# HGRN's f and q projections computed with the tokens stationary and turned through DRAM, in a hybrid decoder trunk

## The chip, the cores and the metric

The kernel runs on one core of a Trainium2 chip. The metric is the time of one execution on the device in microseconds (us); a kernel is timed in several runs and the median is given. The profile is that of one execution. It names the engines PE (TensorE, matmuls; PEld is its loading of the stationary operand), DVE (VectorE), ACT (ScalarE), POOL (GpSimd) and SP (SyncE, which here issues the transfers of the weights and of the output).

## The reference, cut to what matters

One layer on x of 256 tokens by 2048 channels. All projections come from one matrix; three mixers A, B and C each make a branch of 1024 channels, which goes through its block of `w_out` and is added to x under a sigmoid gate.

```python
h = rmsnorm(x, norm_w)
proj = h @ w_in
a_q, a_f, a_i, a_z, b_x, b_z, c_z, c_xbc, c_dt, gate_logits = split(proj)
# A (HGRN2): 8 heads of 128 channels, chunks of 64 tokens, scanned with a state per head
log_f = logaddexp(log(lb), log1p(-lb) + log_sigmoid(a_f)); k = -expm1(log_f)
b = cumsum(log_f)                                 # within the chunk
decay = exp(where(causal, b[t] - b[s], -inf))
scores = einsum('tk,sk,tsk->ts', a_q, k, decay)
o_a = scores @ a_i + (a_q * exp(b)) @ state
o_a = rmsnorm(o_a, hgrn_norm_w) * silu(a_z)
...                                               # B: convolution and a gated scan; C: SSD
branches = stack([o_a, o_b, o_c])
x = x + sum_n sigmoid(gate_logits[n]) * (branches[n] @ w_out[n])
return rmsnorm(x, final_norm_w)
```

## The kernel before, in words

**Precision.** Every large product is made of fp32r matmuls with both sides split into a high and a low part, three products in all (high by high, high by low, low by high). The input times `norm_w` is there as `hT`, 16 slices of 128 channels by 2 parts by 256 tokens. The weights come as tiles `raw` of 128 x 2048 values (1 MB, issued by SP, three buffers). `split(h)` (L394) takes half a tile: ACT casts it to `whi` (L408) and DVE subtracts to get `wlo` (L410). Four buffers each (`WB`) let the splitting run ahead of PE.

**Two forms of block.** `tok_block` (L504) has the tokens stationary: for each of 16 slices and each half of the tokens, three matmuls (L516 to L518) with 128x128 of `hT` stationary and 512 columns of weights moving; 96 matmuls for 512 columns of the projection, and the result lies as tokens by channels. `chan_block` (L454) has the weights stationary and moves `hT`: for each slice and each of two groups of 128 channels one matmul of 512 columns (both parts of `hT` against `whi`, L465) and one of 256 (L466); 64 matmuls for 256 columns of the projection, and the result lies as channels by tokens. PSUM holds two such blocks (`pp`), so a block must have been emptied by the end of the block after it.

**Emptying.** A channel block of f or q is emptied by `copied` and `joined`: ACT copies one half out of PSUM, DVE adds the other and multiplies by `rstd`. Token blocks whose result must lie by channels are emptied by `turned` (x of B and C) or `silu2` (the z gates): ACT scales into a buffer `gt` (two of them), DVE transposes 32x32 blocks into a second `gt`, and POOL's queue writes it to DRAM; `pads_in` and `gates_in` then read it back by POOL's queue as channels by tokens. `gates` keeps tanh of a merge gate in both `gt` buffers until `merged` has used them.

**Order of the work.** `plan()` (L32) lists the blocks; PE runs them in that order without a pause of its own. All other work is written as generator streams. A model clock (`Clock`, `Streams`) advances PE by a constant of the code (0.64 us for three matmuls) and the other engines by formulas; after each such step `quantum` emits those pieces of streams that fit by the model. A piece marked "p" (matmuls of a stream) is placed in PE's queue only where the model has its inputs ready. The order is fixed in the program; on the chip an engine waits where the model was wrong. Transfers enter the model as a fixed delay in `ready`.

**Stages.** C and B come first, up to about 401 us of the span; then stage A: per i from 0 to 3 the channel blocks a_f and a_q (two heads each), for i 0 and 2 the block a_z, and one merge of branch B (a gate block of 96 matmuls and a `wout` block of 48). Then come four merges of branch A. `a_unit(i)` (L1059) is the stream of two heads: ACT and DVE make the logarithms from f, a scan makes `b`, seven levels of products with exponentials follow, then small matmuls on PE, and the result is split into `boh` and `bol`. Tokens such as "A1", "A2", "ls" let one unit use a set of buffers at a time. The first `wout` block of branch A waits for all four units (`force`, `left[0]`).

**The end.** `last_block` (L522) computes the last `wout` block in three parts (token half 0; then token half 1 in two column halves); `last_merge` adds each to x, sums squares, takes the power -0.5 on POOL and scales rows, which SP writes out (`scaled`, L1318).

Of the kernel before, what the change touches and what calls it, by code (L numbers as in the profile page):

```python
# [277 lines left out]
def trunk(ctx, tc, xT, xtok, w, wdt, wax, prm, heads, cst, msk, fnw, out):  # L278
# [175 lines left out]
    def chan_block(name):  # L454

        h0 = 2 * FIRST[name]
        st.room()
        ps = pp.tile([P, 2, 512], F32, name="ps")
        for q in range(4):
            hi, lo = part(h0 + q)  # L460
            for kk in range(4):
                k = q * 4 + kk
                for ct in range(2):
                    c0 = kk * 256 + ct * 128
                    pe.matmul(ps[:, ct], lhsT=hi[:, c0:c0 + 128], rhs=flat(hT[:, k]), start=k == 0, stop=False)  # L465
                    pe.matmul(ps[:, ct, S:], lhsT=lo[:, c0:c0 + 128], rhs=hT[:, k, 0], start=False, stop=k == KD - 1)  # L466
                spent(h0 + q, kk == 3)
        return ps

# [190 lines left out]
    def joined(o, ps):  # L660

        act.copy(out=o, in_=ps[:, :, S:])
        st.after()
        dve.tensor_tensor(out=o, in0=o, in1=ps[:, :, 0:S], op=ALU.add)
        dve.tensor_tensor(out=o, in0=o, in1=rstd.broadcast_to([P, 2, S]), op=ALU.mult)
# [576 lines left out]
    def copied(pool, ps, tag, name):  # L1242
        yield from st.get(tag, "a")
        if tag == "q":

            t = pool.tile([P, 16, 48], F32, name=tag, bufs=2)
            o, ps, r = t[:, :, 0:32].rearrange("p (c g) s -> p c g s", c=2), ps.rearrange("p c (i g s) -> p c i g s", i=2, g=8), rstd.rearrange("p o (g s) -> p o g s", g=8)
            for c in range(2):
                act.copy(out=o[:, c], in_=ps[:, c, 1])
            st.after()  # L1250
            for c in range(2):
                dve.tensor_tensor(out=o[:, c], in0=o[:, c], in1=ps[:, c, 0], op=ALU.add)
            dve.tensor_tensor(out=o, in0=o, in1=r.broadcast_to([P, 2, 8, 32]), op=ALU.mult)
        else:
            t = pool.tile([P, 512], F32, name=tag, bufs=2)
            joined(t.rearrange("p (c s) -> p c s", c=2), ps)
        ready[name] = (t, ck.end)

# [40 lines left out]
    def last_merge(ps, j, c0, c1):  # L1299
# [6 lines left out]
        for _ in merge_in(ps, 0, 3, j, c0, c1):  # L1306
            if n == 4:
                scaled(0, 0, 512, dve)
        if c1 == 512:
# [2 lines left out]
            gp.tensor_tensor(out=tot[:, 1:2], in0=tot[:, 0:1], in1=fin["half"], op=ALU.pow)
# [1 line left out]
        if j == 1:
            for c, w, on in ((512, 512, act), (1024, 512, act), (1536, 512, act)) if n == 3 else ((0, 256, dve), (1024, 512, act), (256, 256, dve), (512, 512, dve), (1536, 512, dve)):
                scaled(n - 3, c, w, on)

    def scaled(j, c, w, on):  # L1318
# [6 lines left out]
        nc.sync.dma_start(out=out[j, :, c:c + w], in_=o)  # L1325

    for name, kind, arg in PLAN:
# [11 lines left out]
        elif kind == "C":  # L1339
            if name == "a_f0":  # L1340
# [5 lines left out]
            ps = chan_block(name)  # L1346
            what, i = name[:3], name[-1]
            st.empty(copied(A[2], ps, what[2], name))
            if what == "a_f":
                st.add(a_unit(int(i)))  # L1350
        elif kind == "T":
# [150 lines left out]
```

## Time and profile before

| what | value |
|---|---|
| median of 3 runs (lowest to highest) | 828.19 us (827.52 to 828.86) |
| the profiled execution's own time | 828.65 us |
| its span, and granted clock of PE | 826.7 us, 0.995 |
| busy share: PE, DVE, ACT, POOL | 98%, 74%, 58%, 11% |
| PE's first block begins, last matmul begins | 5.6 us, 816.8 us |

The profiled execution took 1.95 us more than its span, and 0.46 us more than the median. Matmuls are pipelined: a matmul of 512 columns is shown 389 ns long while the next begins 227 ns later, so durations of PE rows overlap, and what a block costs is read from the starts. A row of the timeline gives start, duration, engine, line, operation, output and inputs, and in brackets the idle time before it and what ended it. Most operations of ACT and DVE stand under L154, the line of a helper, and are told apart by their tiles.

### The profile page before, as it was taken

The numbers are of one execution on the slowest core, as the hardware profiler recorded it, in microseconds if no ns is written. First come the engines' busy times: TensorE is split into PE (matmuls) and PEld (weight loads), VectorE is DVE, ScalarE is ACT, GpSimd is POOL, SyncE is SP. The second block draws the span as 40 slices with busy tenths as digits, with TensorE's granted clock in tenths as the row PEclk, the third lists the DMA queues.
The fourth block names the chain that finished last, engine by engine and source line by source line (L and its number), as shares of the span: only waits on it lengthen the run. The fifth ranks groups of instructions, "written<-read, shape, count | busy, mean of one in ns | idle before, by whom it ended". The sixth has DMA issues, their size and how long they took to land.

```text
span 826.7 us, 12101 instructions
## 1 busy us (share of the span) xinstructions
PE 811.6 (98%) x4677; PEld 678.2 (82%) x4677; DVE 610.2 (74%) x968; ACT 479.0 (58%) x653; POOL 91.7 (11%) x175
## 2 busy tenths in 40 slices
PE   8999999999999999999999999999999999999995
PEld 8978788888888888888888888888888888888884
DVE  6577658888778787878586888689778868656463
ACT  6556445565665676666466565747745673744443
POOL 0000514410520052000100200000020000000000
PEclk9999999999999999999999999999999999999998
DMA  9947676864776587655545744553574555565522
GB/s 339 360 158 249 201 254 215 272 223 179 242 248 246 193 259 250 216 183 190 207 153 204 224 168 171 204 205 125 194 243 153 172 204 186 200 211 201 203 102 101
DMA packets 30088, 171.63 MB, mean 208 GB/s; under 512 B 4960, under 2 KB 5504, under 8 KB 11984
## 3 DMA queue, kind: packets, MB, share of 16 engines
q1 hardware_dynamic: 23360, 153.63, 52.8%
q0 software_dynamic: 6528, 17.16, 7.0%
q8 instruction: 36, 0.59, 0.3%
q10 hardware_dynamic: 144, 0.09, 0.1%
q14 instruction: 20, 0.16, 0.1%
HBM read 163.50 MB, written 7.36 MB: 207 GB/s over the span
## 4 chain that ended last, share of the span: by engine, by line
PE 93%; DVE 2%; DMA 2%; ACT 1%; issue 1%; SPq 0%; POOL 0%; POOLq 0%; DVEq 0%; ACTq 0%
PE ps L516 25%; PE ps L518 25%; PE ps L517 25%; PE ps L465 7%; PE ps L466 3%; PE pmt L154 3%; PE ps L478 2%; DMA xc_t<-xT 1%; DMA xd<-gt 1%; PE pmt L981 1%; DVE wlo L410 1%; ACT whi L408 1%; DVE sc L154 0%; ACT l L154 0%; PE ps L536 0%
## 5 line engine op out<-in xcount | busy, mean ns | idle before, releaser
L410 DVE TENSOR_TENSOR wlo<-raw,whi 128x1024 fp32r<-128x1024 f32 x275 | 333.0, 1220 | 164.3 <-ACT whi L408 162.2
L408 ACT CAST whi<-raw 128x1024 fp32r<-128x1024 f32 x275 | 286.9, 1050 | 285.4 <-PE ps L518 201.3
L516 PE MATMUL ps<-whi,hT 128*128 128x512 f32 x768 | 301.2, 392 | 0.0
L517 PE MATMUL ps<-wlo,hT 128*128 128x512 f32 x768 | 299.1, 389 | 0.0
L518 PE MATMUL ps<-whi,hT 128*128 128x512 f32 x768 | 299.1, 389 | 0.0
L516 PEld LDWEIGHTS ps<-whi,hT 128*128 128x128 f32 x768 | 144.2, 188 | 30.6 <-issue 1.1
L518 PEld LDWEIGHTS ps<-whi,hT 128*128 128x128 f32 x768 | 144.2, 188 | 30.1
L517 PEld LDWEIGHTS ps<-wlo,hT 128*128 128x128 f32 x768 | 144.2, 188 | 29.3
L465 PE MATMUL ps<-hT,whi 128*128 128x512 f32 x256 | 90.6, 397 | 0.0
L466 PE MATMUL ps<-hT,wlo 128*128 128x256 f32 x256 | 71.7, 280 | 0.0
L516 PE MATMUL ps<-whi,boh 128*128 128x512 f32 x176 | 69.2, 393 | 0.0
L518 PE MATMUL ps<-whi,bol 128*128 128x512 f32 x176 | 68.6, 390 | 0.0
L517 PE MATMUL ps<-wlo,boh 128*128 128x512 f32 x176 | 68.5, 389 | 0.0
L465 PEld LDWEIGHTS ps<-hT,whi 128*128 128x128 f32 x256 | 48.0, 188 | 11.3
L466 PEld LDWEIGHTS ps<-hT,wlo 128*128 128x128 f32 x256 | 48.3, 189 | 0.2
L719 POOL DMA_DIRECT2D cpad<-xd x64 | 38.7, 672 | 16.7 <-DMA xd<-gt 7.5
L518 PEld LDWEIGHTS ps<-whi,bol 128*128 128x128 f32 x176 | 33.0, 188 | 6.9
L516 PEld LDWEIGHTS ps<-whi,boh 128*128 128x128 f32 x176 | 33.1, 188 | 6.6
L517 PEld LDWEIGHTS ps<-wlo,boh 128*128 128x128 f32 x176 | 33.1, 188 | 6.5
L154 ACT ACTIVATE gt<-ps,rtok 128x512 f32<-128x512 f32 x44 | 29.5, 683 | 8.7 <-PE ps L518 6.9
L127 ACT ACT_TABLE_LOAD x26 | 33.4, 1283 | 1.6 <-PEq L1495 1.2
L686 POOL DMA_DIRECT2D zd<-gt x12 | 6.7, 560 | 241.1 <-DVE gt L154 177.9
(241 smaller groups left out, 691.2 us busy)
## 6 DMA issues: line engine op xcount, KB each, us to landing
raw<-w SPq DMA_DIRECT2D x137, 1024.0 KB, 4.8
zd<-gt POOLq DMA_DIRECT2D x12, 256.0 KB, 2.7
gz<-zd POOLq DMA_DIRECT2D x48, 64.0 KB, 4.9
raw<-w SPq DMA_DIRECT2D x5, 512.0 KB, 9.0
xsq<-xtok SPq DMA_DIRECT2D x2, 1024.0 KB, 10.9
brd<-sums POOLq DMA_DIRECT2D x4, 512.0 KB, 5.8
xd<-gt POOLq DMA_DIRECT2D x8, 256.0 KB, 2.7
cpad<-xd POOLq DMA_DIRECT2D x64, 32.0 KB, 4.3
```

The source lines that it names most:

```text
L127: self.eng.preload_act_table_set(self.set)
L154: return f(*a, **k)
L408: nc.scalar.copy(out=hi, in_=raw[:, sl])
L410: nc.vector.tensor_tensor(out=lo, in0=raw[:, sl], in1=hi.bitcast(F32), op=ALU.subtract)
L465: pe.matmul(ps[:, ct], lhsT=hi[:, c0:c0 + 128], rhs=flat(hT[:, k]), start=k == 0, stop=False)
L466: pe.matmul(ps[:, ct, S:], lhsT=lo[:, c0:c0 + 128], rhs=hT[:, k, 0], start=False, stop=k == KD - 1)
L478: pe.matmul(ps[:, ct], lhsT=(hi, lo)[i][:, c0:c0 + 128], rhs=hT[:, q * 4 + kk, j], start=q == 0 and n == 0, stop=q == 3 and n == last)
L516: pe.matmul(pss[j], lhsT=hi_ap(k, j), rhs=hi[:, sl], start=k == 0, stop=False)
L517: pe.matmul(pss[j], lhsT=hi_ap(k, j), rhs=lo[:, sl], start=False, stop=False)
L518: pe.matmul(pss[j], lhsT=lo_ap(k, j), rhs=hi[:, sl], start=False, stop=k == nk - 1)
L719: gp.dma_start(out=t[32 * q:32 * q + 32, ct, 3:].rearrange("p (j i s) -> p j i s", j=2, i=4), in_=zd[q, 2 * u + ct])
L981: pe.matmul(o, lhsT=wp[:, a, ct, g], rhs=xp[:, b, ct], start=u == 0, stop=u == 2)
```

## The change

- f and q of a pair of heads become one token block `x_a{i}` of 512 columns (256 of f, 256 of q); `chan_block`, `copied` and `joined` go. The number of weight tiles stays.
- The block is emptied by `turned`; a new stream `heads_in` reads it back with 8 transfers for f and 8 for q. Within f the channels of the two heads now lie interleaved in groups of 32 tokens, and `a_unit` undoes this on the way (`head`, `plain`), writing the log of the gate to a new tile `lf` in the buffer of `l1`; "ls" is given back earlier, "A1" later.
- `turned` scales in place in PSUM and transposes from PSUM, with one `gt` buffer where there were two; `silu2` likewise, and its added wait of 2.5 us of the model goes.
- The plan of stage A: the merge of branch B comes one block later (x_a0, a_z0, x_a1, merge 0, x_a2, a_z1, merge 1, x_a3, merges 2 and 3).
- The end: rows of token half 0 are scaled and written earlier; the square sum of the last part is one DVE operation (`tensor_tensor_reduce`) where it was ACT's and an addition; the last rows are scaled in six pieces, two of them by ACT, which issues their transfers on its own queue.

```diff
     for i in range(4):
-        c(f"a_f{i}", (A_F + i * 256, 256))
-        c(f"a_q{i}", (A_Q + i * 256, 256))
+        t(f"x_a{i}", (A_F + i * 256, 256), (A_Q + i * 256, 256))
         if i % 2 == 0:
             t(f"a_z{i // 2}", A_Z + i * 256)
-        merge(1, i)
+        if i:
+            merge(1, i - 1)
+    merge(1, 3)
...
     def silu2(ps, name):
...
-            dve.scalar_tensor_tensor(out=u, in0=ps[j], scalar=1.0, in1=u, op0=ALU.add, op1=ALU.mult)
-            if j == 1:
-                st.cur.t = max(st.cur.t, ck.end) + 2.5
-                yield "v"
-
-            r = gpool.tile([P, 512], F32, name="gt")
-            dve.transpose(out=r.rearrange("p (q w s) -> p w q s", q=4, w=4), in_=u.rearrange("p (w q s) -> p w q s", q=4, w=4))
-            gp.dma_start(out=zds[name][:, j], in_=r)
+            dve.scalar_tensor_tensor(out=ps[j], in0=ps[j], scalar=1.0, in1=u, op0=ALU.add, op1=ALU.mult)
+
+            dve.transpose(out=u.rearrange("p (q w s) -> p w q s", q=4, w=4), in_=ps[j].rearrange("p (w q s) -> p w q s", q=4, w=4))
+            gp.dma_start(out=zds[name][:, j], in_=u)
...
     def turned(ps, name):
...
-            u = gpool.tile([P, 512], F32, name="gt")
-            act.activation(out=u, in_=ps[j], func=AF.Copy, scale=rtok[:, 0, j:j + 1])
+            act.activation(out=ps[j], in_=ps[j], func=AF.Copy, scale=rtok[:, 0, j:j + 1])
             yield "v"
             r = gpool.tile([P, 512], F32, name="gt")
-            dve.transpose(out=r.rearrange("p (q w s) -> p w q s", q=4, w=4), in_=u.rearrange("p (w q s) -> p w q s", q=4, w=4))
+            dve.transpose(out=r.rearrange("p (q w s) -> p w q s", q=4, w=4), in_=ps[j].rearrange("p (w q s) -> p w q s", q=4, w=4))
...
+    def heads_in(name, i):
+
+        yield from flagged(name)
+        zd = zds.pop(name).rearrange("(i c) j (q w s) -> q w c j i s", i=4, q=4, w=4)
+        yield from st.get("f", "")
+        f = A[2].tile([P, 512], F32, name="f", bufs=2)
+        f5 = f.rearrange("p (j i w s) -> p w j i s", j=2, i=4, w=2)
+        for q in range(4):
+            for w in range(2):
+                gp.dma_start(out=f5[32 * q:32 * q + 32, w], in_=zd[q, w])
+        ready[f"a_f{i}"] = (f, st.cur.t + 12.0)
...
+        ready[f"a_q{i}"] = (t, st.cur.t + 18.0)
...
-        for h, sl in hs:
-            dve.scalar_tensor_tensor(out=ls[:, sl], in0=ls[:, sl], scalar=lnlb[:, h:h + 1], in1=f[:, sl], op0=ALU.max, op1=ALU.add)
+        lf = a1.tile([P, 512], F32, tag="l1", name="lf")
+        for ct, (h, sl) in enumerate(hs):
+            dve.scalar_tensor_tensor(out=plain(lf, ct), in0=head(ls, ct), scalar=lnlb[:, h:h + 1], in1=plain(f, ct), op0=ALU.max, op1=ALU.add)
         st.put("f")
-        st.put("A1")
+        st.put("ls")
...
     def last_merge(ps, j, c0, c1):
...
+        if n == 3 and j == 1:
+
+            scaled(0, 512, 512, act, nc.sync)
+            scaled(0, 1024, 512, dve, nc.sync)
...
+            scaled(0, 1536, 512, act, nc.sync)
...
+            dve.tensor_tensor_reduce(out=g, in0=xa, in1=xa, scale=1.0, scalar=tot[:, 0:1], op0=ALU.mult, op1=ALU.add, accum_out=tot[:, 0:1])
...
+        if j == 0:
+            scaled(0, 0, 512, act, nc.sync)
+        elif n == 4:
+            for c, w, on, q in ((512, 512, act, nc.scalar), (1536, 256, act, nc.scalar), (0, 256, dve, nc.sync), (256, 256, dve, nc.sync), (1024, 512, dve, nc.sync), (1792, 256, dve, nc.sync)):
+                scaled(1, c, w, on, q)
```

More of the change, by code (lines that the diff above doesn't have):

```diff
@@ L70 @@
 PLAN = plan()
-NT = {"C": 2, "CC": 4, "T": 4, "O": 2}
+NT = {"CC": 4, "T": 4, "O": 2}
 FIRST = {}
@@ L452, in spent @@
         st.quantum()
[L454 to L468, printed above, removed]
     def first_quarter(ps, q, hi, lo, h):
@@ L658, in until @@
         return t
[L660 to L665, printed above, removed]
     zds = {}
@@ L720, in pads_in @@
             ready[part] = (t, st.cur.t + 10.0 + 8.0 * u)
+    def heads_in(name, i):
[8 more added lines that the diff above has]
+        ready[f"a_f{i}"] = (f, st.cur.t + 12.0)
+        yield from st.get("q", "")
+        t = A[2].tile([P, 16, 48], F32, name="q", bufs=2)
+        for q in range(4):
+            for w in range(2):
+                gp.dma_start(out=t[32 * q:32 * q + 32, 8 * w:8 * w + 8, 0:32].rearrange("p (j i) s -> p j i s", j=2), in_=zd[q, 2 + w])
+        ready[f"a_q{i}"] = (t, st.cur.t + 18.0)
     def gates_in(pool, name):
@@ L1086, in a_unit @@
         yield "v"
-        for h, sl in hs:
-            dve.scalar_tensor_tensor(out=ls[:, sl], in0=ls[:, sl], scalar=lnlb[:, h:h + 1], in1=f[:, sl], op0=ALU.max, op1=ALU.add)
+        lf = a1.tile([P, 512], F32, tag="l1", name="lf")
+        for ct, (h, sl) in enumerate(hs):
+            dve.scalar_tensor_tensor(out=plain(lf, ct), in0=head(ls, ct), scalar=lnlb[:, h:h + 1], in1=plain(f, ct), op0=ALU.max, op1=ALU.add)
         st.put("f")
-        st.put("A1")
+        st.put("ls")
         yield from st.get("A2", "v")
@@ L1095, in a_unit @@
         fo = a1.tile([P, 256], F32, name="fo")
-        dve.tensor_tensor_scan(b, cc("scan"), ls, 0.0, op0=ALU.mult, op1=ALU.add)
-        act.activation(out=fo, in_=halves(ls, 1)[1][:, :, 0], func=AF.Exp)
-        st.put("ls")
+        dve.tensor_tensor_scan(b, cc("scan"), lf, 0.0, op0=ALU.mult, op1=ALU.add)
+        act.activation(out=fo, in_=halves(lf, 1)[1][:, :, 0], func=AF.Exp)
+        st.put("A1")
         dve.tensor_tensor(out=c, in0=lk, in1=b, op=ALU.subtract)
@@ L1240, in trunk @@
     xacc, fin, gts = {}, {}, {}
[L1242 to L1257, printed above, removed]
     def values(ps, i):
@@ L1305, in last_merge, with scaled @@
             dve.tensor_scalar(out=tot[:, 0:1], in0=tot[:, 0:1], scalar1=D * EPS, scalar2=None, op0=ALU.add)
-        for _ in merge_in(ps, 0, 3, j, c0, c1):
-            if n == 4:
-                scaled(0, 0, 512, dve)
+        cl = slice(3 * 512 + c0, 3 * 512 + c1)
+        xa, g = xacc[0][:, j, cl], gts[j][:, c0:c1]
+        dve.scalar_tensor_tensor(out=g, in0=g, scalar=1.0, in1=ps[:, c0:c1], op0=ALU.add, op1=ALU.mult)
+        dve.scalar_tensor_tensor(out=xa, in0=g, scalar=0.5, in1=xa, op0=ALU.mult, op1=ALU.add)
+        if n == 3 and j == 1:
+            scaled(0, 512, 512, act, nc.sync)
+            scaled(0, 1024, 512, dve, nc.sync)
+            t = fin["pool"].tile([P, 512], F32, name="fsq", bufs=2)
+            act.activation(out=t[:, c0:c1], in_=xa, func=AF.Square, accum_out=fin["fs"][:, j, n:n + 1])
+            scaled(0, 1536, 512, act, nc.sync)
+        elif j == 0:
+            t = fin["pool"].tile([P, 512], F32, name="fsq", bufs=2)
+            act.activation(out=t, in_=xa, func=AF.Square, accum_out=fin["fs"][:, j, n:n + 1])
+            dve.tensor_tensor(out=tot[:, 0:1], in0=tot[:, 0:1], in1=fin["fs"][:, j, n:n + 1], op=ALU.add)
+        else:
+            dve.tensor_tensor_reduce(out=g, in0=xa, in1=xa, scale=1.0, scalar=tot[:, 0:1], op0=ALU.mult, op1=ALU.add, accum_out=tot[:, 0:1])
         if c1 == 512:
-            dve.tensor_tensor(out=tot[:, 0:1], in0=tot[:, 0:1], in1=fin["fs"][:, j, n:n + 1], op=ALU.add)
             gp.tensor_tensor(out=tot[:, 1:2], in0=tot[:, 0:1], in1=fin["half"], op=ALU.pow)
         weigh(3, j, c0, c1)
[L1314 to L1318, printed above, removed]
+        if j == 0:
[3 more added lines that the diff above has]
+                scaled(1, c, w, on, q)
+    def scaled(j, c, w, on, queue):
         o, r = xacc[0][:, j, c:c + w], fin["tot"][:, j, 1:2]
@@ L1324, in scaled @@
             act.activation(out=o, in_=o, func=AF.Copy, scale=r)
-        nc.sync.dma_start(out=out[j, :, c:c + w], in_=o)
+        queue.dma_start(out=out[j, :, c:c + w], in_=o)
     for name, kind, arg in PLAN:
@@ L1338, in trunk @@
             branch_out(1)
-        elif kind == "C":
-            if name == "a_f0":
+        elif kind == "T":
+            if name == "x_a0":
                 st.force(lambda: left[1] == 0 and not st.list)
@@ L1345, in trunk @@
                 branch_out(0)
[L1346 to L1351, printed above, removed]
             ps = tok_block(name, h_hi, h_lo, KD)
@@ L1354, in trunk @@
                 st.empty(values(ps, int(name[-1])))
+            elif name[:3] == "x_a":
+                st.empty(turned(ps, name))
+                st.add(heads_in(name, int(name[3])))
+                st.add(a_unit(int(name[3])))
             elif name[:2] == "x_":
```

21 lines of the change are left out of this document (10 added, 11 removed).

## The prediction

> **What bounds the kernel now.** I read first the page's span, busy times and the chain of work that ended last.
>
> ```profile
> span 826.7 us, 12101 instructions
> PE 811.6 (98%) x4677; PEld 678.2 (82%) x4677; DVE 610.2 (74%) x968; ACT 479.0 (58%) x653; POOL 91.7 (11%) x175
> ...
> PE 93%; DVE 2%; DMA 2%; ACT 1%; issue 1%; SPq 0%; POOL 0%; POOLq 0%; DVEq 0%; ACTq 0%
> ```
>
> PE is busy all the way and makes 93% of the chain. So time is won only where PE streams less, where PE waits, and in the tail after its last matmul. Next the view of waits, of PE alone; its columns are time in all, times, longest.
>
> ```profile
> PE pmt L154 <- DVE ce L154: 1.8, 1, 1.8
> ...
> PE pmt L154 <- DVE sc L154: 1.1, 2, 0.9
> ```
>
> ```profile
> ACT whi L408 <- PE ps L518: 201.3, 143, 3.9
> ```
>
> After its start PE waits three times: 1.8 us once for `ce` (stage C), 1.1 us in two waits for `sc` (units of stage A). The second fence, from the view of all waits, says that the splitting of weights is ahead: ACT waits for PE to give a buffer back, not PE for ACT.
>
> **Part 1: what PE streams for f and q.** The timeline of PE gives the step of each form: first a channel block (stage A), then a token block.
>
> ```profile
> 403.76 0.40 PE L465 MATMUL ps<-hT,whi 128*128 128x512 f32 x1
> ...
> 408.71 0.40 PE L465 MATMUL ps<-hT,whi 128*128 128x512 f32 x1
> ```
>
> ```profile
> 429.82 0.39 PE L518 MATMUL ps<-whi,hT 128*128 128x512 f32 x1
> ...
> 432.54 0.39 PE L518 MATMUL ps<-whi,hT 128*128 128x512 f32 x1
> ```
>
> ```profile
> L465 PE MATMUL ps<-hT,whi 128*128 128x512 f32 x256 | 90.6, 397 | 0.0
> L466 PE MATMUL ps<-hT,wlo 128*128 128x256 f32 x256 | 71.7, 280 | 0.0
> ```
>
> Between the first two rows lie 14 pairs (L465 and L466): 4.95 us / 14 = 0.3536 us a pair. Between the other two lie 12 matmuls: 2.72 / 12 = 0.2267 us each. There are 256 pairs in all (the page's count): 256 x 0.3536 = 90.5 us. They become 4 blocks of 96 matmuls: 384 x 0.2267 = 87.1 us. Removed 90.5, added 87.1: **-3.4 us**, all of it on the path. Both forms move the same columns (64 pairs of 768 columns, or 96 matmuls of 512, are 49,152 for each i); only the number of matmuls falls, from 512 to 384. So the gain is a fixed cost of some 27 ns for each of 128 matmuls, and no fewer columns.
>
> [...]
>
> **Part 2: the wait for `ce`.** Timelines of DVE and of PE around it:
>
> ```profile
> 82.35 1.22 DVE L410 TENSOR_TENSOR wlo<-raw,whi 128x1024 fp32r<-128x1024 f32 x1
> 88.53 0.71 DVE L154 STREAM_TRANSPOSE gt<-gt 128x512 f32<-128x512 f32 x1 [4.96 <-DMA xd<-gt]
> ```
>
> ```profile
> 92.84 0.39 PE L518 MATMUL ps<-whi,hT 128*128 128x512 f32 x1
> 95.06 0.44 PE L154 MATMUL pmt<-ce,xdt 128*64 128x256 f32 x2 [1.84 <-DVE ce L154]
> ```
>
> This is `turned` for x_c0. It takes four `gt` buffers in turn from a pool of two, so the second transpose must wait till the first half has left for DRAM: DVE stands still for 4.96 us, and `xdt`, `ce` and the splits are queued behind it. With the scaling done in PSUM each half takes one buffer, and nothing is in the way. What follows on DVE can come 4.96 us earlier, and PE needs 1.84 of it; 3.1 us are left for what then waits for ACT's next split, whose turn PE sets. **-1.8 us.** What is late next there is PE itself. At the other blocks emptied so the same wait is shorter and no PE wait stands behind it: nothing.
>
> **Part 3: emptying.** From the answers for the tiles f, q and gt (minimum, median, maximum in ns):
>
> ```profile
> L154 ACT COPY f<-ps x4: 573/578/580, 413.6 to 638.2; 128x512 f32<-128x512 f32 x4
> L154 DVE TENSOR_TENSOR f<-f,ps x4: 680/682/689, 414.9 to 639.7; 128x512 f32<-128x512 f32 x4
> L154 DVE TENSOR_TENSOR f<-f,rstd x4: 691/693/694, 415.6 to 640.4; 128x512 f32<-128x512 f32 x4
> ```
>
> ```profile
> L154 ACT COPY q<-ps x8: 354/371/377, 424.9 to 651.9; 128x256 f32<-128x256 f32 x8
> L154 DVE TENSOR_TENSOR q<-q,ps x8: 414/416/422, 426.6 to 652.7; 128x256 f32<-128x256 f32 x8
> L154 DVE TENSOR_TENSOR q<-q,rstd x4: 691/692/693, 427.4 to 653.1; 128x512 f32<-128x512 f32 x4
> ```
>
> ```profile
> L154 ACT ACTIVATE gt<-ps,rtok x44: 669/682/692, 79.6 to 806.4; 128x512 f32<-128x512 f32 x44
> ...
> L154 DVE STREAM_TRANSPOSE gt<-gt x20: 703/706/712, 81.5 to 604.1; 128x512 f32<-128x512 f32 x20
> ```
>
> For each i DVE loses 0.68 + 0.69 + 2 x 0.42 + 0.69 = 2.9 us and gains two transposes, 1.4: over four, -6 us. ACT loses 0.58 + 2 x 0.37 = 1.3 and gains 2 x 0.68: nothing. A transpose that reads PSUM, an ACT result written to PSUM and DVE writing PSUM in `silu2` have no row. The nearest are the DVE additions that read PSUM (682 ns) against the same size from SBUF (693): so 0.68 to 0.71. At twice that, the eight transposes of stage A cost 5.6 us of DVE, about what DVE has gained. The strided halves in `a_unit` keep count and size. All this is on engines with room:
>
> ```profile
> 400.00:720.00 320.00, 318.94 (x2310) 267.42 (x2309) 246.97 (x450) 192.85 (x278) 11.64 (x22) 1.00 0.54 186
> ```
>
> The window of stage A shows PE busy 318.94 of 320 us, DVE 246.97, ACT 192.85. Part 3: 0, hidden beside PE's stream.
>
> **Part 4: the way through DRAM.** Per i the change adds two writes and 16 reads on POOL's queue. The nearest rows are those of x_b1, with the same pieces (32 KB, runs of 32 tokens), from the timelines of DVE and POOL and the list of transfers:
>
> ```profile
> 287.26 0.71 DVE L154 STREAM_TRANSPOSE gt<-gt 128x512 f32<-128x512 f32 x1 [1.77 <-DMA xd<-gt]
> ```
>
> ```profile
> 288.27 0.55 POOL L703 DMA_DIRECT2D xd<-gt  x1 [5.35 <-DVE gt L154]
> ...
> 291.54 4.86 POOL L719 DMA_DIRECT2D cpad<-xd  x8 [2.61 <-DMA xd<-gt]
> ```
>
> ```profile
> cpad<-xd POOLq DMA_DIRECT2D x64, 32.0 KB, 4.3
> ```
>
> The transpose ends at 287.97, the eighth read is issued by 296.40 and lands 4.3 us later, 300.7: f is there 12.7 us after its transpose, q after eight more issues (4.86 us) at about 17.6. The program orders the unit's first step 12 of its own us later, q's use 18; its PE runs at 0.64 us for three matmuls where the chip takes 0.68, so this is 12.8 and 19.1 us of the chip. They fit to a tenth and to 1.5 us. Queued behind the unit's first step on ACT are the splits; buffers for four halves, each used for 12 matmuls (2.72 us), cover three halves less one split (DVE 1.22, ACT counted alike): 8.2 - 2.4 = 5.8 us. Part 2's DVE stall of 4.96 made PE wait for `ce`, not for a split, which agrees. Cost: 0.
>
> [...]
>
> **Part 5: unit 3 and the join.** The first `wout` block of A needs all four units:
>
> ```profile
> 428.89 1.22 DVE L154 TENSOR_TENSOR_SCAN b<-cs,ls 128x512 f32<-128x512 f32 x1
> ...
> 493.93 0.68 DVE L154 TENSOR_TENSOR bol<-osq,boh 128x512 fp32r<-128x512 f32 x1
> ...
> 511.49 1.22 DVE L154 TENSOR_TENSOR_SCAN b<-cs,ls 128x512 f32<-128x512 f32 x1
> ...
> 712.87 0.69 DVE L154 TENSOR_TENSOR bol<-osq,boh 128x512 fp32r<-128x512 f32 x1 [0.69 <-ACT boh L154]
> ```
>
> ```profile
> 740.33 0.39 PE L516 MATMUL ps<-whi,boh 128*128 128x512 f32 x1
> ```
>
> From unit 0's scan to the last unit's end (713.56) are 284.7 us, with 26.8 us to spare before the join. Now unit 0 begins later: its block ends after 96 x 0.2267 = 21.8 us, not 11.3 (32 pairs), and f takes 12.7 us where copy and two DVE passes took 2.7 (413.6 to 416.3, the f rows): some 21 us. The join comes 3.4 us earlier. That would leave 2.4. But the units follow one another through "A2", and between unit 0's end and unit 1's scan lie 16.9 us (494.61 to 511.49), because unit 1's f came late. Now x_a1 ends two blocks, 43.5 us, after x_a0, well within unit 0's 66 us (428.89 to 494.61), so that gap closes and about 19 us are to spare. No price; the strips of DVE between units are filled, which can shift pieces for PE (rivals).
>
> **Part 6: the tail.** Timelines of DVE, ACT and POOL after the last matmul, SP's last two transfers, and the DMA in a window:
>
> ```profile
> 817.55 0.42 DVE L154 SCALAR_TENSOR_TENSOR xacc<-gt,xacc 128x256 f32<-128x256 f32 x1
> ```
>
> ```profile
> 818.07 0.42 ACT L154 ACTIVATE fsq<-xacc 128x256 f32<-128x256 f32 x1 [0.41 <-DVE xacc L154]
> ```
>
> ```profile
> 818.86 0.67 POOL L1312 TENSOR_TENSOR tot<-tot,half 128x1 f32<-128x1 f32 x1 [4.00 <-DVE tot L154]
> ```
>
> ```profile
> 821.34 0.90 SPq L1325 DMA_DIRECT2D out_dram<-xacc  x2
> ```
>
> ```profile
> 822.00:823.00 1.00, 0.00 (x0) 0.00 (x0) 0.00 (x0) 0.00 (x0) 0.00 (x0) 0.50 1.03 370
> ```
>
> From the end of `xacc` (817.97) to POOL are 0.89 us through ACT and a DVE addition. The fused DVE sum has no row; nearest is the 256-element DVE pass, 0.42, so 0.5 with the hand-over; twice that pass would eat the gain. -0.35. Against it, ACT now scales two pieces of half 0 before the third square sum, which may hold DVE back 0.1. SP's last issue ends at 822.24; with four issues on SP and two on ACT it would end some 0.8 earlier. But at 822 the transfer engines are full (370 GB/s), and the last 1 MB needs 2.8 us at that rate whoever issues it; so of this I take 0.15. Together **-0.4 us**, from +0.5 to -1.2.
>
> **Sum.** -3.4 - 1.8 - 0.4 = -5.6 us from the profiled execution's 828.65 (span 826.7), so 823.0. That execution was 0.46 above the median, 828.19: **822.6 us**.
>
> **The rivals.**
> *The two waits for `sc` go too* (1.1 us): they hang on where the program sets PE's pieces, and all of stage A is ordered anew. For: DVE has 6 us less. Time: 821.5.
> *New waits of that kind*: eight such places in stage A, the worst was 0.9. Three or four at 0.5 to 0.9 give 1.5 to 3.5 us: 824.1 to 826.1. For: the units close up, and the order of the z and merge blocks around them is new.
> *Columns alone set the price* of part 1, so that it saves nothing: 826.0. Against: the steps above are regular over 14 pairs and 12 matmuls. [...]
> *Slower: f comes late at ACT.* Place: the first step of each unit, ACT waiting for the eight reads with the splits behind it. Price: what exceeds 5.8 us, four times. To use up the 5.6 us gained it must be 5.8 + 1.4 = 7.2 us late, 20 us after the transpose in place of 12.7; at 9 us late it is four times 3.2, so 835.4. Against: the landings of x_b1, and POOL is idle there (11.64 us of 320).
> *The change does not do what it says*: DVE stalls at 82 us all the same, behind some other buffer: 824.4.
>
> **Chances.** Forecast 0.45 (821.9 to 823.4); `sc` waits gone 0.17; new waits 0.22; columns alone 0.04; DVE stall kept 0.05; f late or the join missed 0.04; the rest, 0.03, is a tail at the outer ends. A measurement of this kernel tells about 0.2% from no change, 1.7 us. Faster by more than that, below 826.5: 0.92. Within: 0.04. Slower: 0.04. The range goes from 820.2 (both `sc` waits gone, tail near -1.2, and a little) to 826.0 (new waits of 3.4 us).
>
> **What would show it.** Right: no L465; the four x_a blocks stepping at 0.227 us; no DVE idle on xd near 83 us and no wait of PE for `ce`; f landing 12 to 13 us after its transpose; POOL's last power about 0.5 us after `xacc`; PE waits of at most 1 to 2 us in stage A. Wrong: PE waiting for whi, wlo or `sc` by more than 4 us between 400 and 720; ACT idle on f for over 6 us; a gap before the first `wout` block of A; transposes from PSUM much over 0.7 us.

## The result and the profile after

The changed kernel takes 832.92 us (median of six runs, 831.88 to 836.83) against 828.42 us for the kernel before (six runs, 827.47 to 828.86): a ratio of 1.0057 [1.0042, 1.0072]. It is 4.5 us slower, where the prediction had it 5.6 us faster. The profiled execution took 831.97 us. The head of its page, then its chain of work:

```profile
span 830.2 us, 11965 instructions
PE 811.4 (98%) x4549; PEld 672.4 (81%) x4549; DVE 605.7 (73%) x957; ACT 486.4 (59%) x652; POOL 134.4 (16%) x247
...
PE 84%; issue 4%; DMA 4%; DVE 3%; ACT 3%; POOL 2%; SPq 0%; POOLq 0%; ACTq 0%; DVEq 0%
```

PE has 128 instructions fewer and is shown busy as long as before. Its share of the chain fell from 93% to 84%: DMA, ACT, DVE and POOL now stand in it. The view of waits of PE, then of ACT (time in all, times, longest):

```profile
PE pmt L152 <- ACT whi L406: 3.9, 2, 2.6
PE pmt L152 <- DVE sc L152: 2.0, 1, 2.0
...
PE ps L499 <- DVE wlo L408: 0.8, 2, 0.5
```

```profile
ACT l L152 <- DMA q<-xd: 10.1, 4, 3.5
```

`ce` is gone from the list. In its place PE waits 6.7 us in stage A, and ACT, which before waited for f once (2.26 us, for DVE's part of the emptying), stands 10.1 us at the first step of the four units (`l` is computed from f; the row names q's transfers, which share POOL's queue).

The window of stage A that the prediction showed, now of the changed kernel:

```profile
400.00:720.00 320.00, 313.26 (x2158) 257.43 (x2157) 238.02 (x435) 197.66 (x275) 54.75 (x94) 0.99 0.56 193
```

PE works 313.26 of 320 us where it was 318.94, at a clock of 0.99 in place of 1.00. DVE has 9 us less to do than before (238.02) and ACT 5 us more (197.66), so neither has become the bound by its work.

**Where the time went**, by the starts of PE's blocks in the two profiled executions:

| stretch | before, us | after, us | difference |
|---|---|---|---|
| to the first token block | 30.89 | 31.22 | +0.33 |
| the next three token blocks (the `ce` wait lies in the third) | 73.37 | 71.43 | -1.94 |
| the rest of C, and B | 297.04 | 297.77 | +0.73 |
| stage A, to the start of its last block | 404.31 | 409.58 | +5.27 |
| last block and end | 21.1 | 20.2 | -0.9 |

The loss is in stage A. Whether the gain of the last row is the change's isn't settled: from the last matmul's start to the end of the span lie 9.9 us before and 9.0 after, but with the new end alone (the run e4_tail, below) 10.0.

Stage A itself. The x_a blocks are what part 1 said. Timeline of PE, first matmul of x_a0 and first of the block behind it:

```profile
400.42 0.39 PE L498 MATMUL ps<-whi,hT 128*128 128x512 f32 x1
...
422.18 0.39 PE L498 MATMUL ps<-whi,hT 128*128 128x512 f32 x1
```

21.76 us for 96 matmuls, 0.2267 each; the two channel blocks took 22.60 (401.30 to 423.90). So 4 x 0.84 = 3.4 us are won, and 8.6 us are lost elsewhere in the stage. The largest piece of the loss is at 491 us. First POOL, with the last transpose of x_a1 on DVE ahead of it (unit 1's f on its way through DRAM):

```profile
470.89 0.71 DVE L152 STREAM_TRANSPOSE gt<-ps 128x512 f32<-128x512 f32 x1
```

```profile
471.89 0.56 POOL L673 DMA_DIRECT2D xd<-gt  x1 [2.15 <-DVE gt L152]
477.00 4.86 POOL L701 DMA_DIRECT2D f<-xd  x8 [4.55 <-issue]
```

POOL stands 4.55 us between the write and the first read. The bracket names no releaser here; in units 0 and 3, where the same gap is 3.26 and 4.98 us, it names the landing of the write (2.61 us at x_b1, in the prediction's row). The eight issues take the 4.86 us that the prediction gave them, and f is there when ACT goes on. ACT's timeline, then DVE's:

```profile
485.83 0.63 ACT L152 ACTIVATE l<-f 128x512 f32<-128x512 f32 x1 [2.50 <-DMA q<-xd]
486.49 1.30 ACT L152 ACTIVATE l<-l 128x512 f32<-128x512 f32 x2
487.69 0.25 ACT L152 COPY sc<-pmt 128x128 f32<-128x128 f32 x1
487.84 1.05 ACT L406 CAST whi<-raw 128x1024 fp32r<-128x1024 f32 x1
```

```profile
487.82 0.69 DVE L152 SCALAR_TENSOR_TENSOR ls<-f,l 128x512 f32<-128x512 f32 x1 [3.24 <-ACT l L152]
...
489.53 0.88 DVE L152 SCALAR_TENSOR_TENSOR lk<-f,ln1lb,l 128x256 f32<-128x256 f32 x2
490.33 0.22 DVE L152 TENSOR_TENSOR dg<-pmt,cs 128x64 f32<-128x64 f32 x1
...
492.81 0.79 DVE L152 COPY sc<-dg 32x64 f32<-32x64 f32 x4
```

ACT has f 14.2 us after the end of its transpose (485.83 less 471.60; units 0, 2 and 3: 14.0, 12.9, 15.5). ACT stands 2.50 us. Behind ACT, DVE stands 3.24 us at unit 1's `ls`. And behind `ls` in DVE's order is not a split but the last work of unit 0: `dg` and `sc`, the scores of its head, whose matmul already stands at the front of PE's queue:

```profile
490.76 0.39 PE L500 MATMUL ps<-whi,bol 128*128 128x512 f32 x1
493.74 1.40 PE L152 MATMUL pmt<-sc,vt 128*128 128x256 f32 x4 [2.59 <-ACT whi L406]
494.79 0.78 PE L498 MATMUL ps<-whi,boh 128*128 128x512 f32 x1
495.36 0.63 PE L499 MATMUL ps<-wlo,boh 128*128 128x512 f32 x1
495.79 0.63 PE L500 MATMUL ps<-whi,bol 128*128 128x512 f32 x1
```

The bracket names ACT's `whi`, but the last cast before it had ended at 488.9; what ends at 493.60, 0.14 us before PE goes on, is DVE's `sc`. So this is a wait for `sc`. And it costs more than its 2.59 us: the next matmuls of 512 columns step by up to 0.57 us, not 0.23. The windows around it (the third number from the right is the clock granted to PE):

```profile
493.50:494.00 0.50, 0.26 (x1) 0.29 (x2) 0.47 (x2) 0.48 (x2) 0.00 (x0) 0.98 0.00 0
494.00:497.00 3.00, 3.00 (x25) 2.06 (x28) 2.77 (x4) 2.73 (x4) 0.00 (x0) 0.50 0.00 0
497.00:497.50 0.50, 0.50 (x48) 0.50 (x42) 0.00 (x0) 0.50 (x2) 0.00 (x0) 0.61 0.00 0
497.50:498.00 0.50, 0.50 (x69) 0.50 (x59) 0.47 (x1) 0.21 (x1) 0.00 (x0) 1.00 0.35 98
```

After the wait the clock is at half (0.50) for 3.4 us, while PE works: another 1.7 us. The kernel before had no such stretch in stage A (1.00). Two more waits of this kind follow for unit 1's head (1.28 and 2.04 us, at 555 and 565 us), without a drop of the clock (1.00), and 0.8 us for `wlo` in unit 3.

The sum of stage A: 404.31 - 3.36 (part 1) + 6.15 (waits, from start to start of the matmuls around them: 7.53 us after, 1.38 before) + 1.70 (half clock) = 408.8; measured 409.58. The remaining 0.8 lies spread over the stretches with small matmuls and was not followed further.

### The profile page after: what moved, and what is told of

It is laid out like the page before. It is cut to its first block, busy times and chain, and to the rows that moved or that the text cites. A ratio compares the mean times of both kernels' runs of the same rounds, so it can differ in the third digit from the quotient of the medians.

```text
span 830.2 us, 11965 instructions
## 1 busy us (share of the span) xinstructions
PE 811.4 (98%) x4549; PEld 672.4 (81%) x4549; DVE 605.7 (73%) x957; ACT 486.4 (59%) x652; POOL 134.4 (16%) x247
## 4 chain that ended last, share of the span: by engine, by line
PE 84%; issue 4%; DMA 4%; DVE 3%; ACT 3%; POOL 2%; SPq 0%; POOLq 0%; ACTq 0%; DVEq 0%
PE ps L498 26%; PE ps L499 26%; PE ps L500 26%; PE pmt L152 3%; PE ps L460 2%; DMA q<-xd 2%; POOL f L701 1%; DMA xc_t<-xT 1%; ACT whi L406 1%; PE pmt L969 1%; DMA xd<-gt 1%; DMA wx<-wax 1%; ACT l L152 1%; POOL gz L718 1%; DVE wlo L408 0%
## 5 line engine op out<-in xcount | busy, mean ns | idle before, releaser
L498 PE MATMUL ps<-whi,hT 128*128 128x512 f32 x896 | 351.8, 393 | 0.0
L499 PE MATMUL ps<-wlo,hT 128*128 128x512 f32 x896 | 348.9, 389 | 0.0
L500 PE MATMUL ps<-whi,hT 128*128 128x512 f32 x896 | 348.8, 389 | 0.0
L498 PEld LDWEIGHTS ps<-whi,hT 128*128 128x128 f32 x896 | 168.2, 188 | 35.5 <-issue 1.1
L500 PEld LDWEIGHTS ps<-whi,hT 128*128 128x128 f32 x896 | 168.2, 188 | 35.2
L499 PEld LDWEIGHTS ps<-wlo,hT 128*128 128x128 f32 x896 | 168.3, 188 | 33.8
L673 POOL DMA_DIRECT2D xd<-gt x16 | 8.9, 555 | 225.6 <-DVE gt L152 220.2
L718 POOL DMA_DIRECT2D gz<-zd x48 | 26.2, 553 | 36.9 <-DVE osq L152 15.9
L152 ACT ACTIVATE gt<-ps,rtok 128x512 f32<-128x512 f32 x36 | 24.0, 684 | 8.3 <-PE ps L500 6.9
L701 POOL DMA_DIRECT2D f<-xd x32 | 19.4, 693 | 15.2 <-DMA xd<-gt 8.2
L707 POOL DMA_DIRECT2D q<-xd x32 | 19.9, 774 | 4.1 <-DMA f<-xd 2.9
L152 DVE STREAM_TRANSPOSE gt<-ps 128x512 f32<-128x512 f32 x28 | 19.9, 712 | 0.4
```

The costliest lines, as they stand in the source:

```text
L152: return f(*a, **k)
L498: pe.matmul(pss[j], lhsT=hi_ap(k, j), rhs=hi[:, sl], start=k == 0, stop=False)
L499: pe.matmul(pss[j], lhsT=hi_ap(k, j), rhs=lo[:, sl], start=False, stop=False)
L500: pe.matmul(pss[j], lhsT=lo_ap(k, j), rhs=hi[:, sl], start=False, stop=k == nk - 1)
L701: gp.dma_start(out=f5[32 * q:32 * q + 32, w], in_=zd[q, w])
L707: gp.dma_start(out=t[32 * q:32 * q + 32, 8 * w:8 * w + 8, 0:32].rearrange("p (j i) s -> p j i s", j=2), in_=zd[q, 2 + w])
```

## The experiments

**Theory A**: f lands after ACT has come to a unit's first step; what stands in order behind that step (the `sc` of the unit before, the splits) comes late, and PE waits. Take away f's lateness alone and stage A loses its waits. **Theory B**: the units now close up and the order of the z and merge blocks is new; PE's small matmuls would wait for DVE in this denser order even if f came in time.

**e1_later** tells the program that f and q come later, and changes nothing else.

```diff
-        ready[f"a_f{i}"] = (f, st.cur.t + 12.0)
+        ready[f"a_f{i}"] = (f, st.cur.t + 16.0)
...
-        ready[f"a_q{i}"] = (t, st.cur.t + 18.0)
+        ready[f"a_q{i}"] = (t, st.cur.t + 22.0)
```

> Edit: only the two delays by which the changed kernel orders the use of f and q after their way through DRAM, 12 and 18 of the program's own us, become 16 and 22. Theory A (ACT stands 2 to 3.5 us in front of the unit's first step because f lands late; the copies to sc of the unit before are queued behind it, and PE's small matmuls wait for those): ACT's four waits on f (10.1 us) shrink to under 2 us in all, PE's waits in stage A fall from 8 us to 1 to 3, time 826 to 829. Rival B (the new order of stage A is too dense for DVE, with or without a late f): the waits of ACT go, PE's waits for sc stay at 6 to 9 us, time 831 to 835.

Measured: 846.25 us, 1.0201 [1.0183, 1.0219]. Neither expectation came true. ACT's waits for f are gone, as they should be, but the delay moves every later piece of the units, and these became longer: from the scan to `bol` 69, 82 and 72 us in three of them, where the changed kernel takes 60, 65 and 64. The last unit ends at 731.7 us, and the join comes too early:

```profile
708.13 0.65 PE L152 MATMUL pmt<-ql,kx 128*32 128x128 f32 x8 [7.29 <-DVE ql L152]
713.71 1.62 PE L152 MATMUL pmt<-sc,vt 128*128 128x256 f32 x4 [3.46 <-DVE sc L152]
720.84 1.62 PE L152 MATMUL pmt<-sc,vt 128*128 128x256 f32 x4 [3.46 <-DVE sc L152]
723.86 0.80 PE L1210 MATMUL pmt<-two,onesr 128*128 128x512 f32 x1 [1.40 <-ACT two L152]
```

15.6 us of waits, and from 704.8 to 728.7 us the clock is at half (0.50 in the window from 705 to 725), which takes 6.1 us more of PE's working time. So this kernel says nothing on A or B; it says that the delay in the program is no knob for one wait: it reorders four units.

**e2_static** leaves all instructions in their order and takes away f's lateness alone: f and q are read from an array that has been in DRAM from the start.

```diff
-        zd = zds.pop(name).rearrange(...)
+        zd = (xtok[:, :, 512 * i:512 * i + 512], zds.pop(name))[0].rearrange(...)
```

> Edit: f and q are read by the same 16 transfers from the input x, which is there from the start, instead of from what the block has written; the writes stay, and the order of every instruction on every engine is that of the changed kernel, so only the wait for the written block goes (the values of f and q are then not those of the projection). Theory A: f lands 3 to 5 us earlier, ACT does not wait for it, PE's waits in stage A fall from 8 us to 1 to 3, time 826 to 829. Rival B (the order itself): time 831 to 834, with the waits for sc still there.

Measured: 826.08 us, 0.9965 [0.9953, 0.9978]. ACT doesn't wait for f, PE's waits in stage A fall to 2.5 us (two for `sc`), the clock stays at 1.00, and stage A takes 403.16 us in place of 409.58. Theory A holds and B falls as the main cause; of B the two `sc` waits remain.

**e3_psum** is the kernel before with the new `turned` and `silu2` alone (and, as in the change, eight DRAM buffers `xd` for four); **e4_tail** the kernel before with the new last block alone.

```diff
-            act.activation(out=u, in_=ps[j], func=AF.Copy, scale=rtok[:, 0, j:j + 1])
+            act.activation(out=ps[j], in_=ps[j], func=AF.Copy, scale=rtok[:, 0, j:j + 1])
...
-            dve.scalar_tensor_tensor(out=u, in0=ps[j], scalar=1.0, in1=u, op0=ALU.add, op1=ALU.mult)
+            dve.scalar_tensor_tensor(out=ps[j], in0=ps[j], scalar=1.0, in1=u, op0=ALU.add, op1=ALU.mult)
```

> Edit: the kernel before with only the new turned and silu2 (scaling and transposing in PSUM, one gt buffer for each half, no added wait of 2.5). By the step of the prediction: PE's wait of 1.84 us for ce near 93 us goes, so 826.4 to 826.8. From the changed kernel's trace: 2.0 us gained there, 0.7 lost again between 320 and 367 us, where wx stands behind gz on POOL's queue: 827.1. If it does nothing: 828.4.

```diff
+            dve.tensor_tensor_reduce(out=g, in0=xa, in1=xa, scale=1.0, scalar=tot[:, 0:1], op0=ALU.mult, op1=ALU.add, accum_out=tot[:, 0:1])
...
+            for c, w, on, q in ((512, 512, act, nc.scalar), (1536, 256, act, nc.scalar), ...):
+                scaled(1, c, w, on, q)
```

> Edit: the kernel before with only the new last block (order of scaling, one DVE sum, six last pieces, two of them issued by ACT). The prediction's step: 0.4 us less, 828.0. From the changed kernel's trace, where last matmul to end of span is 9.03 us and was 9.92: 0.9 less, 827.5.

Measured: e3_psum 827.74 us, 0.9985 [0.9976, 0.9994]; the wait for `ce` is gone. e4_tail 829.28 us, 1.0008 [0.9999, 1.0017]: alone, the new end brings no gain that shows.

**e5_f4 and e6_f16** change in how many transfers f is read, and nothing in the order of PE, ACT and DVE. In e5_f4 both halves of a 64-token run go in one transfer: four of 64 KB. In e6_f16 it is sixteen of 16 KB.

```diff
-        f5 = f.rearrange("p (j i w s) -> p w j i s", j=2, i=4, w=2)
+        f5 = f.rearrange("p (j i m) -> p j i m", j=2, i=4)
         for q in range(4):
-            for w in range(2):
-                gp.dma_start(out=f5[32 * q:32 * q + 32, w], in_=zd[q, w])
+            gp.dma_start(out=f5[32 * q:32 * q + 32], in_=zf[q])
```

> Edit: the changed kernel with f read in 4 transfers of 64 KB (runs of 256 B) in place of 8 of 32 KB; the order on PE, ACT and DVE is unchanged. Theory A (what counts is when f lands, since ACT stands before the unit's first step and PE's small matmuls of the unit before wait for what is queued behind): four issues of 0.6 us less, so f lands some 2.4 us earlier, ACT's four waits on f fall from 10.1 us to 1 to 3, PE's waits in stage A from 8 us to 3 to 4, time 827 to 829. Rival C (the write to DRAM and its landing set the time, the number of reads does not): 832 to 833.

```diff
-            for w in range(2):
-                gp.dma_start(out=f5[32 * q:32 * q + 32, w], in_=zd[q, w])
+            for w in range(2): gp.dma_start(out=f5[32 * q:32 * q + 32, w, 0], in_=zd[q, w, :, 0])
+            for w in range(2): gp.dma_start(out=f5[32 * q:32 * q + 32, w, 1], in_=zd[q, w, :, 1])
```

> Edit: the changed kernel with f read in 16 transfers of 16 KB; the order on PE, ACT and DVE is unchanged. The suspected cost made larger. Theory A: eight more issues of 0.6 us, f lands some 4.9 us later; ACT's four waits rise from 10 to 30 us, and three of the four (units 1 to 3, with small matmuls of the unit before in PE's queue) pass it on to PE: 832.9 + 3 x 4.9, so 843 to 848. Rival C: 832 to 834. By the prediction's cover of 5.8 us for the splits alone the waits of about 7.5 us would cost 4 x 1.7: 839.

Measured: 826.03 us, 0.9963 [0.995, 0.9976], and 843.11 us, 1.017 [1.0153, 1.0188]. The waits of PE, first of e5_f4, then of e6_f16:

```profile
PE pmt L152 <- DVE sc L152: 2.5, 2, 1.6
```

```profile
PE pmt L152 <- ACT whi L406: 11.0, 2, 8.2
PE ps L498 <- ACT whi L406: 2.4, 1, 2.4
...
PE ps L499 <- DVE wlo L408: 0.8, 1, 0.8
```

The first step of the four units on ACT, in e5_f4 (no bracket: no wait) and in e6_f16:

```profile
440.11 0.63 ACT L152 ACTIVATE l<-f 128x512 f32<-128x512 f32 x1
483.69 0.62 ACT L152 ACTIVATE l<-f 128x512 f32<-128x512 f32 x1
544.26 0.62 ACT L152 ACTIVATE l<-f 128x512 f32<-128x512 f32 x1
629.19 0.62 ACT L152 ACTIVATE l<-f 128x512 f32<-128x512 f32 x1
```

```profile
442.89 0.63 ACT L152 ACTIVATE l<-f 128x512 f32<-128x512 f32 x1 [2.88 <-DMA f<-xd]
491.71 0.63 ACT L152 ACTIVATE l<-f 128x512 f32<-128x512 f32 x1 [8.13 <-DMA q<-xd]
556.37 0.63 ACT L152 ACTIVATE l<-f 128x512 f32<-128x512 f32 x1 [3.43 <-DMA f<-xd]
647.74 0.63 ACT L152 ACTIVATE l<-f 128x512 f32<-128x512 f32 x1 [6.35 <-DMA f<-xd]
```

With the changed kernel between them this is a series:

| transfers for f | ACT waits for f | half clock, PE's working time lost | stage A | median |
|---|---|---|---|---|
| 4 | 0 us | 0 us | 403.15 us | 826.03 us |
| 8 (the change) | 10.1 us | 1.7 us | 409.58 us | 832.92 us |
| 16 | 20.8 us | 4.7 us | 420.78 us | 843.11 us |

From 8 to 4 transfers stage A wins 6.4 us: 4.7 of waits (7.53 to 2.82 from start to start) and 1.7 of clock. That is the cause, shown with the change's own order. Both runs went the way of theory A and not of C, but the sizes were off. e5_f4 came out 1 us below its range. e6_f16 lies in its range (843 to 848) in part by luck: ACT's waits came to 20.8 us and not 30, and the half clock, which stood in no sum, made up for it. The series also says what covers a wait and what doesn't. Unit 0's wait (2.26 us in the change, 2.88 in e6_f16) costs PE nothing: no other unit's small matmuls are queued, only splits, and their buffers hold that long. Unit 3's costs little, 1.15 us of 3.46, and 3.56 of 6.35 in e6_f16, through `whi` and `wlo`: the buffers cover 2.3 to 2.8 us. Unit 1's 2.50 us cost 2.75 and then 1.7 of clock: `sc` has no cover at all.

**e7_turned** is the kernel before with the new `turned` alone; **e8_f4_oldsilu** is e5_f4 with the old `silu2`. They are to say which of the two edits costs the 0.7 us in the rest of C and in B. In `silu2`'s new order `wx` stands on POOL's queue behind eight issues of the gates (4.38 us in the changed kernel), and PE waits for `wp`, which is made from it.

```diff
-            act.activation(out=u, in_=ps[j], func=AF.Copy, scale=rtok[:, 0, j:j + 1])
+            act.activation(out=ps[j], in_=ps[j], func=AF.Copy, scale=rtok[:, 0, j:j + 1])
```

> Edit: the kernel before with only the new turned, silu2 as before. If the 0.7 us lost between 320 and 367 us with both edits comes from silu2's new order (wx behind gz on POOL's queue), it is not lost here: PE's wait for ce goes (2.0 us) and nothing is added, 826.6 to 827.0. If it comes from turned, the same 827.7 as with both.

```diff
-            dve.scalar_tensor_tensor(out=ps[j], in0=ps[j], scalar=1.0, in1=u, op0=ALU.add, op1=ALU.mult)
+            dve.scalar_tensor_tensor(out=u, in0=ps[j], scalar=1.0, in1=u, op0=ALU.add, op1=ALU.mult)
+            if j == 1:
+                st.cur.t = max(st.cur.t, ck.end) + 2.5
+                yield "v"
...
+            r = gpool.tile([P, 512], F32, name="gt")
```

> Edit: the changed kernel with f read in 4 transfers and silu2 as before. Theory A: as with 4 transfers alone, less the 0.7 us between 320 and 367 us: 826 to 828.5; the order of stage A shifts a little around the z blocks, which can add or take a wait of 1 to 2 us.

Measured: e7_turned 827.53 us, 0.9978 [0.9969, 0.9987], against 0.9985 for e3_psum: the intervals overlap, so the times don't decide between the two expectations, and the traces don't either. PE's wait for `wp` is 0.2 us with the new `silu2` (the change, e3_psum) and absent with the old one (e7_turned, e8_f4_oldsilu). But the rest of C and B take 297.04 and 297.07 us with both edits out (before, e4_tail), 297.58 and 297.28 with the new `turned` alone (e7_turned, e8_f4_oldsilu), and 297.63 to 298.61 in the nine profiles with both. So a part of the loss is there without the new `silu2` too, profiles with the same code differ by 1 us, and the cause of the 0.7 us stays open. e8_f4_oldsilu 826.57 us, 0.9967 [0.9955, 0.998]: its stage A starts at 400.05 us in place of e5_f4's 400.88 and takes 404.13 us in place of 403.15. ACT waits 3.62 us there for the last unit's f, and PE 3.1 us where it was 2.5; that the one brings the other was not tried.

**e9_f4_early, e10_f4_late and e11_f4_oldplan** start from e5_f4. The first two set the program's delays 1.5 us down and up; the last puts the merges of branch B back directly behind each pair.

```diff
-        ready[f"a_f{i}"] = (f, st.cur.t + 12.0)
+        ready[f"a_f{i}"] = (f, st.cur.t + 10.5)
...
-        ready[f"a_q{i}"] = (t, st.cur.t + 18.0)
+        ready[f"a_q{i}"] = (t, st.cur.t + 16.5)
```

> Edit: f in 4 transfers, and the program orders the use of f and q 1.5 of its own us earlier (10.5 and 16.5). Theory A: f now lands before ACT needs it, with an unknown margin; if that is under 1.6 us, ACT waits again by up to 1.6 us a unit and PE by up to 3 us in all. The 2.5 us that PE still waits for sc depend on where the order puts pieces and can fall or rise by 1 to 2 us. 824.5 to 829.

```diff
-        ready[f"a_f{i}"] = (f, st.cur.t + 12.0)
+        ready[f"a_f{i}"] = (f, st.cur.t + 13.5)
...
-        ready[f"a_q{i}"] = (t, st.cur.t + 18.0)
+        ready[f"a_q{i}"] = (t, st.cur.t + 19.5)
```

> Edit: f in 4 transfers, and the program orders the use of f and q 1.5 of its own us later (13.5 and 19.5). No wait for f. If the units only shift by 1.5 us they make the join (unit 3 ended 27 us before it): 824.5 to 827.5. If what cost 13 us with delays of 16 and 22 (each unit 8 to 17 us longer, the fourth not ready at the join) sets in gradually, some of it shows: units longer by 2 to 6 us, time still 825 to 828 as long as the join is made.

```diff
-        if i:
-            merge(1, i - 1)
-    merge(1, 3)
+        merge(1, i)
```

> Edit: f in 4 transfers, and the merges of branch B again directly after each pair of heads (x_a0, a_z0, merge 0, x_a1, merge 1, and so on). Then between the end of x_a3 and the join lie one merge and one gate block, some 60 us of PE with the small matmuls, and unit 3 took 82 us from its f to its end and some 20 from block end to f: the join is missed by 20 to 40 us, of which PE loses what it cannot fill: 840 to 865. If the place of the merges does not matter: 826 to 828.

Measured: 839.94 us, 1.0131 [1.0108, 1.0153]; 825.27 us, 0.9952 [0.9939, 0.9964]; 840.75 us, 1.0137 [1.0123, 1.0151]. **e10_f4_late is faster than both kernels**, 0.5% faster than the one before (from e5_f4 it can't be told, the intervals overlap): PE's waits for `sc` are 1.6 us in three, and stage A takes 402.41 us. e9_f4_early missed what was expected of it. ACT waits only 0.69 us for f, but the units come in another rhythm (unit 0 takes 73.5 us from scan to `bol`), unit 3 ends at 724.1, and the block ahead of the join takes 34.07 us where e10_f4_late's takes 26.56. In e11_f4_oldplan that block takes 40.36 us, for the same reason: with the merges early there is less PE work left to cover the last units. So with these delays the later merges of the change are needed.

## Why the prediction was wrong

The forecast of 822.6 us (820.2 to 826.0) missed by 10.3 us. In the spans of the profiled executions it is 9.1 us (830.2 for 826.7 - 5.6), and 8.7 of that is stage A (5.27 lost where 3.4 were to be won): 6.4 from one step, 1.4 from new waits for `sc`, and 0.8 not followed.

**Part 4, "Cost: 0", failed.** It costs 6.4 us of stage A (409.58 to 403.15, eight transfers to four), in four errors. The landing: 12.7 us was taken from x_b1, and ACT had f after 12.9 to 15.5, with up to 4.98 us between the write and the first read where x_b1 had 2.61. The due time: 12.8 us was worked out from the program's 12, but ACT stood at the step 11.1 to 12.0 us after the transpose (the times above less its waits), so even the landing as forecast would have been 0.7 to 1.6 us late in every unit. The cover: "5.8 us" counted four buffers and one split, but two more passes of `l` (1.30 us for the two) and at times a table load of ACT (1.28) stand behind the wait too, and the series shows 2.3 to 2.8 us. The largest error: "Queued behind the unit's first step on ACT are the splits" left out what waits one engine further. DVE's `ls` waits for ACT, the `sc` of the unit before waits behind `ls`, and PE's small matmul waits for `sc` with no cover, since the program sets it where its clock thinks `sc` is ready. The slow rival had the right place (f late at ACT) and the wrong price: what exceeds 5.8 us would have been zero here. At a chance of 0.04 it was set far too low; a fit of 12.7 to 12.8 us was no margin at all.

**The clock** stood in no term. Behind the wait of 2.59 us at 491 us it was at 0.50 for 3.4 us, which cost 1.7 us beyond the wait.

**Part 1** was right: 22.60 to 21.76 us, four times, 3.4 us. The rival "columns alone" is out.

**Part 2** was right in its place (-1.94 for -1.8; DVE's transposes now stand at 81.83 and 83.83 us with one split between them). Not foreseen was that 0.7 us is given back in the rest of C and in B, for a cause that stays open; e3_psum and e7_turned won 1.2 and 1.8 us by their ratios (0.0015 and 0.0022 of 829).

**Part 3** was right. The transposes from PSUM, minimum, median, maximum in ns:

```profile
L152 DVE STREAM_TRANSPOSE gt<-ps x28: 706/710/718, 81.8 to 621.1; 128x512 f32<-128x512 f32 x28
```

710 against 706 from SBUF; DVE's busy time fell from 610.2 to 605.7 us.

**Part 5** read the wrong row, and its "no price" came out by luck. 740.33 starts A's second `wout` block; the first, which is the join, starts one gate block earlier. Timelines of PE before, then of PE and DVE in the changed kernel:

```profile
707.69 0.39 PE L516 MATMUL ps<-whi,boh 128*128 128x512 f32 x1
```

```profile
712.08 0.39 PE L498 MATMUL ps<-whi,boh 128*128 128x512 f32 x1
...
720.24 0.39 PE L498 MATMUL ps<-whi,boh 128*128 128x512 f32 x1
```

```profile
717.26 0.69 DVE L152 TENSOR_TENSOR bol<-osq,boh 128x512 fp32r<-128x512 f32 x1 [0.69 <-ACT boh L152]
```

The block takes the heads in order and reaches the last unit's two with its 37th matmul, the row at 720.24 (715.85 before). The last `bol` ends at 717.95 (713.56 before). So 2.3 us were to spare in both kernels, not 26.8, and the "27 us" in the expectation of e10_f4_late is the same misreading. With so little, an order that makes the units longer can miss the join: the gate block ahead of it takes 26.6 us in both kernels, and 46.8, 34.1 and 40.4 in e1_later, e9_f4_early and e11_f4_oldplan, 7 to 20 us more.

**Part 6** is not settled. Timelines of DVE and POOL at the end:

```profile
822.09 0.42 DVE L152 SCALAR_TENSOR_TENSOR xacc<-gt,xacc 128x256 f32<-128x256 f32 x1
822.55 0.48 DVE L152 CUSTOM_DVE_ANT_0 gt<-xacc,tot 128x256 f32<-128x256 f32 x1
822.97 0.08 DVE L152 DVE_READ_ACCUMULATOR2_ANT tot<- 128x1 f32 x1
```

```profile
823.13 0.79 POOL L1306 TENSOR_TENSOR tot<-tot,half 128x1 f32<-128x1 f32 x1 [3.88 <-DVE tot L152]
```

From the end of `xacc` (822.51) to POOL are 0.62 us where it was 0.89, but `xacc` itself comes 0.15 us later behind the third square sum, and the power takes 0.79 where it took 0.67. From the last matmul's start to the end of the power it is 2.75 us in both kernels, so the fused sum wins nothing. What follows, the scaling and writing of the rows, takes 7.1 to 7.2 us in the three profiles with the old end, and 6.1 to 6.3 in eight with the new one, but 6.8 in e2_static and 7.2 in e4_tail, and e4_tail's time over its runs shows no gain. So some 0.9 us may be won there; the one run made for it doesn't show it.

**The rival "new waits"** was there in part: with f in time, PE still waits 2.5 us for `sc` in the new order, 1.4 more than before. With it the forecast would have been about 824; e5_f4, at 826.03, is 0.4% faster than before.

What stays open: why 1.5 us less of delay makes the units so much longer, where 1.5 more does not. In e1_later's unit 1 the seven levels take 34 us in place of 18, with unit 2's logarithm and an emptying between them; that is read from the order and was not tried by itself.

## What to carry to other kernels

When a step begins to wait for a transfer, follow what the program has put behind it through every engine until PE's next matmul (here 2.50 us of ACT, 3.24 of DVE and 2.59 of PE), not only to the nearest buffer: cover that holds for one consumer (here splits, 2.3 to 2.8 us) says nothing of another (small matmuls set by the program's clock, here none). A landing time that fits its due time to a tenth is no margin. Here four larger transfers in place of eight gave one, and whether that helps is seen by changing the number of transfers with the order kept. A changed delay in a planner isn't that experiment, since it gives another order of everything behind it.

## What the runs showed of the hardware

Some waits of PE in stage A came with a stretch at half clock. Behind those of 1.28 and 2.04 (the change) and 1.57 us (e5_f4) the clock stayed at 1.00; those of 2.42 (e9_f4_early), 2.59 (the change) and 2.83 us (e6_f16) came with 3.4 us at 0.50 each, which began between 0.4 us before the wait's end and 1.1 us after it. So did one of 2.38 us with another of 0.76 close behind it (e6_f16). The longest, 8.20 us (e6_f16), came with 6.8 us at 0.50, from 3.9 us before its end. In e6_f16 the windows behind the wait of 2.83 us, which ended at 564.27:

```profile
563.00:565.00 2.00, 0.73 (x2) 0.67 (x3) 1.90 (x7) 1.98 (x4) 0.00 (x0) 0.72 0.00 0
565.00:567.00 2.00, 2.00 (x7) 1.26 (x5) 2.00 (x4) 1.99 (x3) 0.00 (x0) 0.50 0.03 8
567.00:569.00 2.00, 2.00 (x107) 1.79 (x107) 1.93 (x4) 0.86 (x2) 0.00 (x0) 0.92 0.38 57
```

In e1_later, where one wait follows another, the clock stays at half from 704.8 to 728.7 us (0.50 in the window from 705 to 725).

For f, the number of transfers on POOL's queue counted more than the bytes of each: 0.61 us of issue apiece (eight in 4.86 us in the change, four in 2.44 in e5_f4, both for unit 1), so that four of 64 KB were all issued 2.4 us sooner than eight of 32 KB, and they landed as fast (the list of transfers has 2.8 us from issue to landing, and 3.1 for the eight).
